# Hybrid decoder layers on one Trainium2 core: window attention moved beside the up projections, latent attention beside retention's projections, output weights prepared before retention's products

## The chip, the cores and the metric

The kernel runs on one core of one Trainium2 chip. The metric is the device time of one execution in microseconds (us). The kernel is a single launch; all weights come from device memory (HBM) during the execution.

## The reference, cut to what matters

Two decoder layers on 256 tokens of width 1024, all in float32. One input projection feeds three mixers; their outputs, concatenated, go through one output projection, a residual and a layer norm; then a router picks 2 of 16 experts for each token.

```python
(r_q, r_k, r_v, r_g, s_q, s_k, s_v, c_q, c_kv, k_rope) = jnp.split(x @ w_in[l], splits, axis=-1)
rq, rk = rope(r_q, pos), rope(r_k, pos)                      # 4 heads of 64
ret_o = retention(rq, rk, r_v, r_g, ret_gn_w[l])             # scores*decay, group norm, * silu(g)
swa_o = sliding_window_sink_attention(s_q, s_k, s_v, sinks)  # 6 query heads, 2 kv heads, band of 128
mla_o = latent_attention(c_q, c_kv, k_rope, ...)             # q = rms(c_q) @ w_uq; k,v = rms(c_kv) @ w_ukv
mix = jnp.concatenate([ret_o, swa_o, mla_o], -1) @ w_out[l]
x = layer_norm(ALPHA * x + mix, ...)
x = layer_norm(ALPHA * x + grouped_moe(x, ...), ...)         # 16 experts, 1024 -> 2x256 -> 1024, top 2
```

## The kernel before, in words

Tokens are two blocks of 128 (`t` = 0, 1). Every float32 product of the projections is done as three products of a shorter format: a weight chunk of 1024 columns is split into a high part (a rounding copy on ACT, L485) and a low part (a subtraction on DVE, L486), and `mm3` issues high·high (L497), low·high (L498) and high·low (L499). Buffers for the high parts are few, so a split waits until PE has finished with an earlier chunk. A block of input columns (`B4`, `B3`, `B2`, `B0`, `B1`) is one `project` of four chunks, 48 products of 512 columns where it is 512 wide.

The order in which the source writes the mixers of a layer is: `B4` (latent keys and values, window values), `B3` (latent queries), `B2` (window queries and keys; `ev2` copies them into `sqT` and the padded key tile `zpad`), the up projections from `w_uq` and `w_ukv` (36 products of 288 columns, then 18 of 256 and 12 of 384), q's transposes, three latent attentions, `B0` (retention's q and k with rotary positions, tile `rqk`), three window attentions, the load of the decay factors (`dec`, on ACT's DMA queue, L821), `B1` (retention's v and gate), retention itself, then the output projection, the routing and the experts.

One attention of two heads (`attend`) is a chain over three engines: PE scores into PSUM; DVE row maxima (L723); ACT exponentials (L729) and, for windows, the sink's (L734); DVE sums and reciprocal (L735, L736); DVE scaling of `p` (L739); PE transposes of `p` (L355); copies to `pt` on DVE and ACT (L213); PE products with the values (L745, L748); the copy into `mixT` in two parts (ACT L750, DVE L751).

Retention's chain is: rotary of `rqk` (DVE L508, L510, and an add on POOL, L511), eight transposes, copies to `rkT` and `zpad`, scores (L846, L847), DVE product with `dec` into `AT` (L849), inner products (L858), group norm (DVE L865, POOL's power L394, POOL's product of gate and scale L871, DVE L872), transposes of `ro`, `mixT`.

A scheduler decides the order of the instructions on each engine from the source and its own costs; each engine then runs its list strictly in the order shown in the next sections' listings. On PE this holds except in a guarded part (output projection, routing, experts), where the written order is kept. The output projection (`outp`, 96 products for both token blocks and both halves `j` of the columns) takes the eight blocks of `mixT` in the order of `order`, its weights' chunks in `OUT_ORDER`; retention's result is blocks 0 and 1, the windows' 2 to 4, latent's 5 to 7. Weights are requested from SP in one stream, with a limit (`pump(LIM[3])`) on how far.

Of the kernel before, what the change touches and what calls it, by code (L numbers as in the profile page):

```python
# [188 lines left out]
def hybrid_decoder_kernel(ctx: ExitStack, tc: tile.TileContext, x, w_in, ret_gn_w, swa_sinks,  # L189
# [86 lines left out]
    OUT_ORDER = (3, 2, 1, 0)  # L276
# [224 lines left out]
    def rope(o, i, cos, sin, nh, d):  # L501
# [9 lines left out]
        gp.tensor_tensor(o, o, tv, op=OP.add)  # L511
# [3 lines left out]
    def mixers(l):  # L515
# [149 lines left out]
        uqs = [split_w(wu, 576 * i, 576) for i in range(3)]  # L665
        for t in range(2):
            for hf in range(2):
                b = mis()
                for i in range(3):
                    mm3(P[:, b, :288], cqH[:, i, 128 * t:128 * t + 128], cqL[:, i, 128 * t:128 * t + 128],  # L670
                        uqs[i][0][:, 288 * hf:288 * hf + 288], uqs[i][1][:, 288 * hf:288 * hf + 288], i == 0, i == 2)
                qh = q[:, t, 3 * hf:3 * hf + 3]
                act.activation(qh, P[:, b, :288].rearrange("p (h d) -> p h d", d=96), AF.Copy, scale=rsq[:, t:t + 1])
                rope(qh[:, :, 64:96], qh[:, :, 64:96], kc(K_COSM + 32 * t, 32), kc(K_SINM + 32 * t, 32), 3, 32)

        uks = []
        for i, (o, ol) in enumerate(((1728, 3264), (2496, 1728))):
            h, lo = hchunk(768), wu.part(ol, ol + 768, F32R)
            w = wu.part(o, o + 768, F32).rearrange("p (h a d) -> p a h d", a=2, d=64)
            hv, lv = (y.rearrange("p (a h d) -> p a h d", a=2, d=64) for y in (h, lo))  # L680
            act.activation(hv, w, AF.Copy)
            dve.tensor_sub(lv, w, f_(hv))
            uks.append((h, lo))
        for pr in range(3):
            b = mis()
            for i in range(2):
                mm3(P[:, b, 0:256], uks[i][0][:, 128 * pr:128 * pr + 128], uks[i][1][:, 128 * pr:128 * pr + 128],
                    ckH[:, i], ckL[:, i], i == 0, i == 1)
            for u in range(2):
                copy(act if u else dve, kT[0:64, 2 * pr + u], P[64 * u:64 * u + 64, b, 0:256])  # L690
# [109 lines left out]

        for pr in range(3):
            window(pr)
        SV.free()
        SQT.free()


# [544 lines left out]
```

## Time and profile before

| | us |
|---|---|
| median of three runs | 526.99 (522.13 to 528.87) |
| the profiled execution | 521.82 |
| its span, first to last instruction | 519.9 |
| from the up projections to the routing, layer 0 / layer 1 | about 45 to 150 / 297 to 402 |
| experts, layer 0 / layer 1 | about 150 to 262 / 402 to 503 |

Times in the trace are counted from the start of the span. A line such as L355 is the line of the kernel that issued the instruction. `DVE` is VectorE, `ACT` ScalarE, `POOL` GpSimd, `SP` SyncE, `PE` TensorE.

### The profile page before, as it was taken

To read this page: it belongs to the slowest core of one execution; us is meant where nothing else is said; L and a number is where in the kernel's file an instruction comes from. 1 tells how busy PE (TensorE), PEld (TensorE's weight loads), DVE (VectorE), ACT (ScalarE), POOL (GpSimd) and SP (SyncE) were. 2 spreads that over 40 slices of the span, in tenths; PEclk is the share of its full clock that TensorE was granted. 3 is DMA by queue.
4 is the path that set the end of the run, shared out by engine and by line. 5 is a ranking of instruction groups with operands and counts; after the bars stand their busy time and mean duration, and the time that the engine had idled before them with its cause. 6 is when DMAs were issued, how large, how long until landed. Compare 5 with 4: busy or idle time off the path is not lost. (4 is left out here: it accounts for less than half of the span.)

```text
span 519.9 us, 8750 instructions
## 1 busy us (share of the span) xinstructions
PE 480.9 (92%) x3328; PEld 301.2 (58%) x3328; DVE 262.8 (51%) x713; ACT 199.4 (38%) x443; POOL 72.9 (14%) x74
## 2 busy tenths in 40 slices
PE   4999999788999999999989999977999999999984
PEld 3999877456855334243379987754677533523331
DVE  4565966855463132322487588576627501422136
ACT  4475754622343132221257485454124511421120
POOL 0022001002220019000003110100121100730000
PEclk9999999979999999999999999997999999999999
DMA  8999629540594999999989942547019779999982
GB/s 267 302 388 383 240 81 301 167 141 0 169 369 146 391 387 387 387 385 386 366 301 388 379 168 81 180 155 249 25 52 337 259 277 385 387 386 385 387 306 81
DMA packets 74164, 140.47 MB, mean 270 GB/s; under 512 B 4571, under 2 KB 11269, under 8 KB 74117
## 3 DMA queue, kind: packets, MB, share of 16 engines
q1 hardware_dynamic: 71264, 136.28, 73.3%
q10 hardware_dynamic: 2852, 3.58, 2.1%
q8 instruction: 28, 0.46, 0.4%
q14 instruction: 20, 0.16, 0.1%
HBM read 138.79 MB, written 1.05 MB: 269 GB/s over the span
## 5 line engine op out<-in xcount | busy, mean ns | idle before, releaser
L1111 PE MATMUL psum<-w_float,xg_float 128*32 128x512 f32 x1024 | 115.0, 594 | 2.1 <-DVE th L1119 2.1
L1111 PEld LDWEIGHTS psum<-w_float,xg_float 128*32 128x32 f32 x1024 | 31.6, 110 | 73.8 <-issue 67.6
L486 DVE TENSOR_TENSOR w_float32r<-w_float,h_r 128x1024 fp32r<-128x1024 f32 (+3 forms) x54 | 58.7, 1104 | 18.5 <-ACT h_r L485 18.4
L1130 PE MATMUL psum<-w_float,aT 128*32 128x512 f32 x512 | 58.4, 594 | 3.5 <-DMA w_float<-in_exp_w_down_dram 2.7
L485 ACT ACTIVATE h_r<-w_float 128x1024 fp32r<-128x1024 f32 (+3 forms) x54 | 51.0, 958 | 26.9 <-PE psum L499 12.4
L1140 DVE TENSOR_TENSOR ye_float32r<-psum,ye_float32r 128x512 fp32r<-128x512 f32 x28 | 19.2, 691 | 60.8 <-ACT ye_float32r L1139 60.8
L394 POOL TENSOR_TENSOR stats<-stats,small 128x1 f32<-128x1 f32 (+2 forms) x18 | 12.8, 710 | 222.8 <-DVE stats L393 222.7
L497 PE MATMUL psum<-h_r,xT_r 128*128 128x512 f32 (+1 forms) x96 | 38.3, 401 | 2.4 <-ACT h_r L485 1.5
L1130 PEld LDWEIGHTS psum<-w_float,aT 128*32 128x32 f32 x512 | 15.8, 110 | 42.1 <-issue 33.7
L499 PE MATMUL psum<-h_r,xT_r 128*128 128x512 f32 (+1 forms) x96 | 38.9, 407 | 0.8 <-DVE stats L393 0.8
L498 PE MATMUL psum<-w_float32r,xT_r 128*128 128x512 f32 (+1 forms) x96 | 38.7, 405 | 0.0
L1139 ACT ACTIVATE ye_float32r<-psum 128x512 fp32r<-128x512 f32 x28 | 16.5, 595 | 56.0 <-PE psum L1130 56.0
L1118 DVE SCALAR_TENSOR_TENSOR th<-th,psum 128x256 f32<-128x256 f32 x16 | 6.7, 421 | 58.1 <-ACT th L1117 58.1
L497 PE MATMUL psum<-xT_r,h_r 128*128 128x256 f32 x112 | 32.1, 288 | 0.0
L499 PE MATMUL psum<-xT_r,w_float32r 128*128 128x256 f32 x112 | 31.6, 284 | 0.0
L498 PE MATMUL psum<-xT_r,h_r 128*128 128x256 f32 x112 | 31.6, 283 | 0.0
L1117 ACT ACTIVATE th<-psum 128x256 f32<-128x256 f32 x16 | 6.1, 383 | 57.4 <-PE psum L1111 56.4
L498 PE MATMUL psum<-w_float32r,mixT_r 128*128 128x512 f32 x64 | 25.2, 394 | 0.0
L355 PE MATMUL psum<-ident_r,p 128*128 128x128 f32 x72 | 13.9, 305 | 10.7 <-DVE p L739 7.8
L729 ACT ACTIVATE p<-p,stats 128x128 f32<-128x128 f32 (+1 forms) x48 | 21.2, 445 | 4.9 <-DVE stats L726 4.9
L1084 ACT ACTIVATE xg_float<-psum,par 128x256 f32<-128x256 f32 x40 | 20.3, 564 | 5.6 <-PE psum L1080 4.9
L497 PEld LDWEIGHTS psum<-h_r,xT_r 128*128 128x128 f32 x96 | 18.7, 196 | 6.3 <-ACT h_r L485 1.9
(227 smaller groups left out, 907.6 us busy)
## 6 DMA issues: line engine op xcount, KB each, us to landing
w_float<-in_exp_w_gate_up_dram SPq DMA_DIRECT2D x64, 1024.0 KB
w_float<-in_exp_w_down_dram SPq DMA_DIRECT2D x32, 1024.0 KB
w_float<-in_w_in_dram SPq DMA_DIRECT2D x24, 512.0 KB
w_float<-in_w_out_dram SPq DMA_DIRECT2D x16, 512.0 KB
w_float<-in_w_in_dram SPq DMA_DIRECT2D x8, 384.0 KB
w_float<-in_w_in_dram SPq DMA_DIRECT2D x8, 288.0 KB
w_float<-in_mla_w_uq_dram SPq DMA_DIRECT2D x6, 288.0 KB
w_float<-in_mla_w_ukv_dram SPq DMA_DIRECT2D x4, 384.0 KB
```

The costliest lines, as they stand in the source:

```text
L355: pe.transpose(o, i, ident[:n, :n] if n != 128 else ident)
L485: first[0] = act.activation(h, w, AF.Copy)
L486: i = (e or dve).tensor_tensor(wl, w, f_(h), op=OP.subtract)
L497: pe.matmul(o, xh, wh, start=first, stop=False)
L498: pe.matmul(o, xh, wl, start=False, stop=False)
L499: pe.matmul(o, xl, wh, start=False, stop=last)
L729: act.activation(sb[u].v(a, z), sb[u].v(a, z), AF.Exp, bias=nb[:, c:c + 1], scale=scale, accum_out=sm[:, c:c + 1])
L1084: act.activation(xg[:, k], P[:, b, 0:256], AF.Identity, scale=g, bias=c)
L1111: pe.matmul(P[32 * e:32 * e + 32, 4 + t, :], xg[t][:, k, 4 * (g % 2) + e], w[:, 512 * e:512 * e + 512], start=k == 0, stop=k == 7, skip_gr ...
L1130: pe.matmul(P[32 * e:32 * e + 32, b, :], R.ATS[t].v(128 * f + 32 * e, 128 * f + 32 * e + 32), w[:, 512 * e:512 * e + 512], start=f == 0, s ...
L1139: act.activation(ys[0], P[:, b, :], AF.Copy)
L1140: last_ye[0] = dve.tensor_sub(ys[1], P[:, b, :], f_(ys[0]))
```

## The change

The windows come straight after `B2`, and the up projections after them in the source, using other PSUM banks (`acc()` in place of `mis()`), so that the scheduler may interleave both. The load of `dec` follows the windows. The latents now stand next to `B0`. Retention's transposes, scores and decay products come before `B1` in the source; the splits of all eight output-weight chunks (both halves) come after `B1` and before retention's inner products, and the output projection of token block 0 for `mixT`'s blocks 2 to 7 is taken out of the guarded part. The rotary add runs on DVE for the wide tiles; group norm's scale is multiplied into `ro` on DVE in place of into the gate on POOL. The transposed normed rows `x1T` get two buffers, and both of block 0's transposes (`turn`) stand together. No product is added or removed.

```diff
--- before.py
+++ after.py
@@ -273,7 +273,7 @@
     def width(blk):
         return sum(n for _, n in blk)
 
-    OUT_ORDER = (3, 2, 1, 0)
+    OUT_ORDER = (1, 2, 3, 0)
     stream = []
     for l in range(DEPTH):
         stream += [("in", l, B4), ("in", l, B3), ("u", l, 0), ("in", l, B2), ("in", l, B0), ("in", l, B1),
@@ -508,7 +508,7 @@
             dve.tensor_mul(tv[:, :, s * h:s * h + h], i[:, :, h - s * h:d - s * h],
                            sin[:, None, s * h:s * h + h].to_broadcast([128, nh, h]))
         dve.tensor_mul(o, i, cb)
-        gp.tensor_tensor(o, o, tv, op=OP.add)
+        (dve if nh * d >= 256 else gp).tensor_tensor(o, o, tv, op=OP.add)
         t2.free()
 
 
@@ -658,54 +658,6 @@
 
         project_T(B2, ev2)
 
-
-        wu = W[("u", l, 0)]
-        V = alloc(768, "mv", within=LAT)
-        v = V.ap.rearrange("p (t h d) -> p t h d", t=2, h=6)
...
-        wfree(("u", l, 0))
-
-
...
         MIX = alloc(4096, "mixT")
         mH, mL = MIX.v(0, 2048, 8, 256, r=True), MIX.v(2048, 4096, 8, 256, r=True)
 
@@ -752,15 +704,6 @@
             for x_ in sb + pts:
                 x_.free()
 
-        def latent(pr):
-            banks = [mis(), mis()]
...
         def window(pr):
             banks = [mis(), mis()]
             kvs = [(2 * pr + u) // 3 for u in range(2)]
@@ -772,6 +715,71 @@
                    [P[:, banks[1], 256 * u:256 * u + 256] for u in range(2)], banks, kc(K_WIN, 256), SWA_SCALE,
                    lambda u, t: sv[:, t, 64 * kvs[u]:64 * kvs[u] + 64], 2 * pr)
 
+
+        for pr in range(3):
+            window(pr)
+        SV.free()
+        SQT.free()
+        DEC = alloc(1024, "dec")
+        nc.scalar.dma_start(DEC.ap, const[:, K_DEC:K_DEC + 1024])
+
+
+        wu = W[("u", l, 0)]
+        V = alloc(768, "mv", within=LAT)
+        v = V.ap.rearrange("p (t h d) -> p t h d", t=2, h=6)
+        uqs = [split_w(wu, 576 * i, 576) for i in range(3)]
+        for t in range(2):
+            for hf in range(2):
+                b = acc()
...
+        for pr in range(3):
+            b = acc()
...
+        for t in range(2):
+            b = acc()
...
+        wfree(("u", l, 0))
+
+
+        QT = alloc(1536, "qT", within=LAT)
+        qT = QT.v(0, None, 6, 256)
+        for h0 in range(0, 6, 2):
+            b = mis()
...
+            copy(dve if h0 == 2 else act, qT[:96, h0:h0 + 2], P[:96, b].rearrange("p (a b) -> p a b", b=256))
+        FRONT.free()
+        def latent(pr):
+            banks = [mis(), mis()]
...
         for pr in range(3):
             latent(pr)
         LAT.free()
@@ -795,33 +803,9 @@
             rope(rqk[:, t].rearrange("p (h d) -> p h d", d=64), p.rearrange("p (h d) -> p h d", d=64),
                  kc(K_COSR + 64 * t, 64), kc(K_SINR + 64 * t, 64), 8, 64)
 
+
+        acc_i[0] = 0
         project(B0, ev0)
-
-
-        for pr in range(3):
-            window(pr)
-        SV.free()
-        SQT.free()
-
-
-        RV = alloc(512, "rv")
-        rv = RV.v(0, None, 2, 256)
-        RG = alloc(512, "rg")
-        rg = RG.v(0, None, 2, 256)
-
...
-        DEC = alloc(1024, "dec")
-        nc.scalar.dma_start(DEC.ap, const[:, K_DEC:K_DEC + 1024])
-        project(B1, ev1)
-        XHL.free()
-        pump(LIM[3])
 
 
         RKT = alloc(512, "rkT")
@@ -836,8 +820,6 @@
             for u in range(2):
                 copy(dve if u else act, qvv[64 * u:64 * u + 64, pr, 256 * u:256 * u + 256], P[64 * u:64 * u + 64, b, 0:256])
         RQK.free()
-        RO = alloc(512, "ro")
-        ro = RO.v(0, None, 2, 256)
         ATs = []
         for pr in range(2):
             AT = alloc(768, "AT")
@@ -849,6 +831,44 @@
             dve.tensor_mul(AT.v(0, 512), P[:, b0, :], DEC.v(512 * pr, 512 * pr + 512))
             dve.tensor_mul(AT.v(512, 768, 2, 128), P[:, b1, 0:256].rearrange("p (u i) -> p u i", u=2),
                            DEC.v(512 * pr, 512 * pr + 512).rearrange("p (u i) -> p u i", u=2)[:, :, 0:128])
+
+        RV = alloc(512, "rv")
+        rv = RV.v(0, None, 2, 256)
+        RG = alloc(512, "rg")
+        rg = RG.v(0, None, 2, 256)
+
+        def ev1(t, p):
...
+        project(B1, ev1)
+        XHL.free()
+
+
+        hb2 = alloc(4096, "h2")
+        order = (2, 3, 4, 5, 6, 7, 0, 1)
+        hs = {}
+
+        def split_out(j, n):
+            c = OUT_ORDER[n]
+            h, lo = split_w(W[("out", l, j)], 1024 * c, 1024,
+                            hb2.part(3072 - 1024 * n, 4096 - 1024 * n, F32R) if j else hb[0].v(1024 * n, 1024 * n + 1024, r=True))
+            for i in range(2):
+                hs[j, 2 * c + i] = h[:, 512 * i:512 * i + 512], lo[:, 512 * i:512 * i + 512]
+
+        for j in range(2):
+            for n in range(4):
+                split_out(j, n)
+        pump(LIM[3])
+
+
+        RO = alloc(512, "ro")
+        ro = RO.v(0, None, 2, 256)
+
         for t in range(2):
             b = mis()
             for h in range(4):
@@ -865,11 +885,11 @@
                 dve.bn_stats(bs, P[:, b, 64 * h:64 * h + 64])
                 dve.bn_aggr(mv[:, h], bs)
             rs = rstd(mv[:, :, 1], LN_EPS, 4)
-            o3, g3 = (y.rearrange("p (h d) -> p h d", d=64) for y in (ro[:, t], rg[:, t]))
+            o3 = ro[:, t].rearrange("p (h d) -> p h d", d=64)
             dve.tensor_tensor(o3, P[:, b, 0:256].rearrange("p (h d) -> p h d", d=64),
                               mv[:, :, 0:1].to_broadcast([128, 4, 64]), op=OP.subtract)
-            gp.tensor_tensor(g3, g3, rs[:, :, None].to_broadcast([128, 4, 64]), op=OP.mult)
             dve.tensor_mul(ro[:, t], ro[:, t], rg[:, t])
+            dve.tensor_tensor(o3, o3, rs[:, :, None].to_broadcast([128, 4, 64]), op=OP.mult)
             b = mis()
             for pr in range(2):
                 transpose(P[:, b, 128 * pr:128 * pr + 128], ro[:, t, 128 * pr:128 * pr + 128])
@@ -881,25 +901,9 @@
 
 
 
-        guard = tc.manual_schedule(engines={mybir.EngineType.PE})
-        guard.__enter__()
-        hb2 = alloc(4096, "h2")
-        R = Routing(l)
-        R.guard = guard
-        order = (6, 7, 5, 4, 2, 3, 0, 1)
-        hs = {}
-
-        def split_out(j, n):
...
-        def outp(t, j, part):
-            bk = 2 * t + j
-            for k in order[4 * part:4 * part + 4]:
-                mm3(P[:, bk, :], mH[:, k, 128 * t:128 * t + 128], mL[:, k, 128 * t:128 * t + 128],
+        def outp(t, j, a, z):
+            for k in order[a:z]:
+                mm3(P[:, 2 * t + j, :], mH[:, k, 128 * t:128 * t + 128], mL[:, k, 128 * t:128 * t + 128],
                     hs[j, k][0], hs[j, k][1], k == order[0], k == order[-1])
 
         def residue(t, j):
@@ -907,21 +911,22 @@
             dve.scalar_tensor_tensor(z, z, ALPHA, P[:, 2 * t + j, :], op0=OP.mult, op1=OP.add)
             ln_stats(t, j, z)
 
-        for n in range(4):
-            split_out(0, n)
-        outp(0, 0, 0)
-        outp(0, 0, 1)
-        residue(0, 0)
-        for n in range(4):
-            split_out(1, n)
-        outp(0, 1, 0)
+        for j in range(2):
+            outp(0, j, 0, 6)
+
+        guard = tc.manual_schedule(engines={mybir.EngineType.PE})
+        guard.__enter__()
+        R = Routing(l)
+        R.guard = guard
+        for j in range(2):
+            outp(0, j, 6, 8)
+            residue(0, j)
+        outp(1, 0, 0, 4)
         R.turn(0, 0)
-        outp(0, 1, 1)
-        residue(0, 1)
+        R.turn(0, 1)
+        outp(1, 0, 4, 6)
         R.products(0, 0)
-        outp(1, 0, 0)
-        R.turn(0, 1)
-        outp(1, 0, 1)
+        outp(1, 0, 6, 8)
         residue(1, 0)
         R.products(0, 1)
         hb[0].free()
@@ -929,9 +934,9 @@
         R.xg = alloc(4096, "xg")
         wfree(("out", l, 0))
         R.choose(0)
-        outp(1, 1, 0)
+        outp(1, 1, 0, 4)
         R.turn(1, 0)
-        outp(1, 1, 1)
+        outp(1, 1, 4, 8)
         residue(1, 1)
         R.products(1, 0)
         R.rank(0)
@@ -962,6 +967,7 @@
             self.ATS = [alloc(256, "aT", within=self.unit) for t in range(2)]
             self.XT = alloc(512, "x1T")
             self.x1 = [[self.XH[t].whole(F32R), Xb.part(1024 * t, 1024 * t + 1024, F32R)] for t in range(2)]
+            self.x1T = [y.part(0, 512, F32).rearrange("p (a b) -> p a b", b=128) for y in (self.XT, self.unit)]
             self.SM = [SMB.v(128 * t, 128 * t + 128) for t in range(2)]
             self.MK = [y.whole(BF) for y in MKB]
             self.bk = []
@@ -979,16 +985,16 @@
 
         def turn(self, t, j):
 
-            self.x1T = self.XT.v(0, None, 4, 128)
+            x1T = self.x1T[j]
             b = 2 + j if t else 4 + j
             for a in range(4):
                 transpose(P[:, b, 128 * a:128 * a + 128], X[t][:, 512 * j + 128 * a:512 * j + 128 * a + 128])
-            copy(act if HC[t][j] == "a" else dve, self.x1T, P[:, b].rearrange("p (a b) -> p a b", b=128))
+            copy(act if HC[t][j] == "a" else dve, x1T, P[:, b].rearrange("p (a b) -> p a b", b=128))
 
         def products(self, t, j):
 
             for k in range(4 * j, 4 * j + 4):
-                pe.matmul(P[:, 0 if t else 6, 0:16], self.x1T[:, k - 4 * j], rwg[:, k, 0:16], start=k == 0, stop=k == 7)
+                pe.matmul(P[:, 0 if t else 6, 0:16], self.x1T[j][:, k - 4 * j], rwg[:, k, 0:16], start=k == 0, stop=k == 7)
 
         def choose(self, t):
 
```

What the scheduler makes of it is seen in each engine's list. In these rows L713 stands for the windows' scores (L770 before), L697 and L700 for their products with the values (L745, L748 before), L828 and L829 for retention's scores (L846, L847 before), L702 and L703 for the copies into `mixT`, L843 and L844 for the gate's.

PE in the up projections, where before only products with `cT_r` stood in a row until the uk ones; now (the changed kernel, `p_47` and `p_48` are the first window's two heads):

```order
L713 MATMUL psum<-zpad_395,sqT_399 128x256
L713 MATMUL psum<-zpad_395,sqT_399 128x512
L713 MATMUL psum<-zpad_395,sqT_399 128x256
L713 MATMUL psum<-zpad_395,sqT_399 128x512
L499 MATMUL psum<-h_r,cT_r 128x288
...
L499 MATMUL psum<-h_r,cT_r 128x288
L355 MATMUL psum<-ident_r,p_47_526 128x128
L497 MATMUL psum<-h_r,cT_r 128x288
L355 MATMUL psum<-ident_r,p_47_526 128x128 x2
L355 MATMUL psum<-ident_r,p_48_532 128x128
```

Between the scores of two windows and the first window's transposes there are 19 products of 288 columns (left out but for the first and last); eight of the 36 stand ahead of the scores.

PE at retention, before. `p_78` to `p_83` belong to the second and third window, `xT_r` products are `B1`'s, `mixT_r` products the output projection's:

```order
L499 MATMUL psum<-h_r,xT_r 128x512
L770 MATMUL psum<-zpad_395,sqT_399 128x256
L355 MATMUL psum<-ident_r,p_78_901 128x128 x3
L355 MATMUL psum<-ident_r,p_79_907 128x128 x3
...
L355 MATMUL psum<-ident_r,rqk_786 128x128 x8
L355 MATMUL psum<-ident_r,p_82_939 128x128 x3
L355 MATMUL psum<-ident_r,p_83_945 128x128 x3
...
L847 MATMUL psum<-zpad_395,rkT_1057 128x256
L846 MATMUL psum<-zpad_395,rkT_1057 128x512 x2
```

and in the changed kernel:

```order
L355 MATMUL psum<-ident_r,rqk_902 128x128 x2
L498 MATMUL psum<-w_3072_4096_float32r,xT_r 128x512
...
L497 MATMUL psum<-h_r,mixT_r 128x512
L355 MATMUL psum<-ident_r,rqk_902 128x128 x6
L497 MATMUL psum<-h_96_3072_4096_float32r,mixT_r 128x512
L498 MATMUL psum<-w_1024_2048_float32r,mixT_r 128x512
...
L498 MATMUL psum<-w_2048_3072_float32r,mixT_r 128x512
L828 MATMUL psum<-zpad_395,rkT_977 128x512
L829 MATMUL psum<-zpad_395,rkT_977 128x256
```

After the last product of `B1` no window is left; six transposes of `rqk` follow one product of the output projection, and nine of its products stand between them and retention's scores.

DVE at the same place in the changed kernel (`w_..._362` and `w_..._356` are chunks of the output weights' first half, 0 and 1):

```order
L703 TENSOR_TENSOR mixT_r<-psum,mixT_r 128x256
L508 TENSOR_TENSOR rope_963<-psum,const_87 128x8x32 x2
L510 TENSOR_TENSOR rqk_902<-psum,const_87 128x512
L511 TENSOR_TENSOR rqk_902<-rqk_902,rope_963 128x512
L486 TENSOR_TENSOR w_0_1024_float32r<-w_0_1024_float_362,h_r 128x1024
L508 TENSOR_TENSOR rope_968<-psum,const_87 128x8x32 x2
L510 TENSOR_TENSOR rqk_902<-psum,const_87 128x512
L844 SCALAR_TENSOR_TENSOR tanh_1065<-tanh_1065,psum 128x256
L511 TENSOR_TENSOR rqk_902<-rqk_902,rope_968 128x512
L845 SCALAR_TENSOR_TENSOR rg_1003<-tanh_1065,gn_389 128x256
L486 TENSOR_TENSOR w_1024_2048_float32r<-w_1024_2048_float_356,h_r 128x1024
```

The add L511 is new on this list, and a split and the gate's L844 stand between the steps of the second rotary.

## Rows read from the trace of the kernel before

**Rows 1.** The page: its span, and the granted TensorE clock in 40 equal slices of the span (9 is 90% of full speed or more).

```profile
span 519.9 us, 8750 instructions
...
PEclk9999999979999999999999999997999999999999
```

**Rows 2.** Busy time of each engine in stretches of the span: start and end, length, then for each engine busy us and instructions, the granted clock, the share of the DMA engines' time and GB/s. Four stretches for the mixers of each layer and one for layer 0's experts.

```profile
45.20:91.10 45.90, 45.74 (x257) 36.84 (x255) 35.45 (x102) 28.17 (x66) 4.93 (x6) 1.00 0.67 234
91.10:105.90 14.80, 9.12 (x50) 5.49 (x49) 11.65 (x46) 9.22 (x33) 0.00 (x0) 0.96 0.57 193
105.90:111.60 5.70, 5.60 (x18) 3.59 (x19) 2.92 (x8) 1.26 (x3) 0.00 (x0) 0.50 0.38 116
111.60:150.10 38.50, 35.85 (x195) 28.68 (x193) 21.03 (x73) 10.75 (x20) 7.77 (x10) 1.00 0.39 133
...
342.60:357.90 15.30, 9.35 (x50) 5.50 (x50) 11.88 (x46) 9.39 (x33) 0.00 (x0) 0.98 0.56 197
357.90:364.10 6.20, 6.16 (x18) 3.86 (x19) 3.01 (x9) 1.64 (x4) 0.00 (x0) 0.50 0.40 115
364.10:402.00 37.90, 35.32 (x194) 28.59 (x192) 20.91 (x73) 10.36 (x19) 7.77 (x10) 1.00 0.39 130
150.10:262.00 111.90, 108.52 (x907) 42.29 (x906) 36.22 (x82) 31.23 (x68) 17.39 (x9) 1.00 0.98 357
```

**Rows 3.** PE's waits in layer 0's mixers (45.2 to 150.1 us): waiting line, the line waited for, total us, times, longest.

```profile
PE psum L355 <- DVE p L739: 3.9, 2, 2.5
PE psum L355 <- DVE ro L872: 1.5, 2, 1.0
PE psum L355 <- ACT h_r L485: 1.3, 1, 1.3
```

**Rows 4.** PE in order of time, layer 0, from the last product of `B1` on: start, us, line, operation; idle time before it and its releaser in brackets.

```profile
97.03 0.39 PE L499 MATMUL psum<-h_r,xT_r 128*128 128x512 f32 x1
97.26 0.59 PE L770 MATMUL psum<-zpad,sqT 128*128 128x256 f32 x2
99.22 1.13 PE L355 MATMUL psum<-ident_r,p 128*128 128x128 f32 x6 [1.37 <-DVE p L739]
...
102.79 0.66 PE L355 MATMUL psum<-ident_r,rqk 128*128 128x128 f32 x4 [0.35 <-DVE mixT_r L751]
105.99 1.56 PE L355 MATMUL psum<-ident_r,p 128*128 128x128 f32 x6 [2.54 <-DVE p L739]
```

**Rows 5.** The second window's chain on DVE and then on ACT, in order of time.

```profile
94.52 0.34 DVE L723 CUSTOM_DVE_ANT_0 p<-psum,const,par 128x128 f32<-128x128 f32 x1
...
98.38 0.17 DVE L735 TENSOR_TENSOR stats<-stats 128x4 f32<-128x4 f32 x1 [1.15 <-ACT stats L734]
...
98.79 1.01 DVE L739 TENSOR_SCALAR p<-p,stats 128x128 f32<-128x128 f32 x4
```

```profile
96.39 0.39 ACT L729 ACTIVATE p<-p,stats 128x128 f32<-128x128 f32 x1
...
98.15 0.19 ACT L734 ACTIVATE stats<-stats 128x4 f32<-128x4 f32 x1
```

**Rows 6.** The end of `B2` and the start of the up projections, in order of time: PE, DVE, ACT; and the two stretches of the up projections in the form of Rows 2.

```profile
45.22 0.30 PE L497 MATMUL psum<-h_r,cT_r 128*128 128x288 f32 x1
45.35 0.29 PE L498 MATMUL psum<-w_float32r,cT_r 128*128 128x288 f32 x1
```

```profile
45.81 0.94 DVE L682 TENSOR_TENSOR w_float32r<-w_float,h_r 128x768 fp32r<-128x768 f32 x1
46.79 0.43 DVE L213 COPY zpad<-psum 64x256 f32<-64x256 f32 x1
```

```profile
47.25 0.38 ACT L213 ACTIVATE zpad<-psum 64x256 f32<-64x256 f32 x1
```

```profile
45.20:50.00 4.80, 4.80 (x39) 4.80 (x38) 3.45 (x13) 3.27 (x8) 0.78 (x2) 1.00 1.05 387
50.00:54.95 4.95, 4.95 (x34) 4.44 (x33) 4.80 (x11) 3.96 (x8) 1.57 (x2) 1.00 0.95 349
```

**Rows 7.** Groups of instructions by line and shape, 40 to 150 us: count, busy us and mean ns, and idle time before them with releasers. DVE, then ACT, then POOL.

```profile
L486 DVE TENSOR_TENSOR w_float32r<-w_float,h_r 128x1024 fp32r<-128x1024 f32 x12 | 14.8, 1231 | 2.3 <-ACT h_r L485 2.3
...
L508 DVE TENSOR_TENSOR rope<-psum,const 128x256 f32<-128x256 f32 x4 | 1.6, 420 | 1.8 <-POOL rqk L511 1.5 <-PE psum L748 0.3
...
L849 DVE TENSOR_TENSOR AT<-psum,dec 128x512 f32<-128x512 f32 x2 | 1.4, 686 | 1.0 <-PE psum L847 1.0
L510 DVE TENSOR_TENSOR rqk<-psum,const 128x512 f32<-128x512 f32 x2 | 1.4, 681 | 0.0
L508 DVE TENSOR_TENSOR rope<-mq,const 128x48 f32<-128x48 f32 x8 | 1.3, 203 | 1.2 <-ACT mq L673 0.6 <-POOL mq L511 0.6
```

```profile
L485 ACT ACTIVATE h_r<-w_float 128x1024 fp32r<-128x1024 f32 x12 | 12.6, 1054 | 5.4 <-PE psum L499 5.1 <-ACT p L729 0.2
```

```profile
L511 POOL TENSOR_TENSOR rqk<-rqk,rope 128x512 f32<-128x512 f32 x2 | 2.6, 1291 | 30.6 <-DVE rqk L510 30.6
L511 POOL TENSOR_TENSOR mq<-mq,rope 128x96 f32<-128x96 f32 x4 | 2.3, 587 | 7.4 <-DVE mq L510 6.6 <-ACT h_r L681 0.8
```

**Rows 8.** Transfers: a stretch at the start of layer 0's experts, in the form of Rows 2; and SP's requests for the output weights in layer 0, in order of time.

```profile
160.00:166.00 6.00, 5.89 (x49) 3.31 (x53) 2.35 (x7) 2.70 (x8) 0.00 (x0) 1.00 0.01 3
```

```profile
40.06 7.26 SPq L308 DMA_DIRECT2D w_float<-in_w_out_dram  x8
```

More of the change, by code (lines that the diff above doesn't have):

```diff
@@ L676, in mixers @@
[L676 to L683, printed above, removed]
-        for pr in range(3):
[L685 to L690, printed above, removed]
@@ L708, in mixers @@
-        FRONT.free()
         MIX = alloc(4096, "mixT")
@@ new lines, in mixers @@
+        uks = []
+        for i, (o, ol) in enumerate(((1728, 3264), (2496, 1728))):
+            h, lo = hchunk(768), wu.part(ol, ol + 768, F32R)
+            w = wu.part(o, o + 768, F32).rearrange("p (h a d) -> p a h d", a=2, d=64)
+            hv, lv = (y.rearrange("p (a h d) -> p a h d", a=2, d=64) for y in (h, lo))
+            act.activation(hv, w, AF.Copy)
+            dve.tensor_sub(lv, w, f_(hv))
+            uks.append((h, lo))
+        for pr in range(3):
+            b = acc()
+            for i in range(2):
+                mm3(P[:, b, 0:256], uks[i][0][:, 128 * pr:128 * pr + 128], uks[i][1][:, 128 * pr:128 * pr + 128],
+                    ckH[:, i], ckL[:, i], i == 0, i == 1)
+            for u in range(2):
+                copy(act if u else dve, kT[0:64, 2 * pr + u], P[64 * u:64 * u + 64, b, 0:256])
@@ new lines, in mixers @@
+        FRONT.free()
+        def latent(pr):
+            banks = [mis(), mis()]
+            for u in range(2):
+                h, b = 2 * pr + u, banks[u]
+                pe.matmul(P[:, b, 0:128], qT[:96, h, 0:128], kT[:96, h, 0:128], start=True, stop=True)
+                pe.matmul(P[:, b, 128:384], qT[:96, h, 128:256], kT[:96, h, :], start=True, stop=True)
+            attend(5 + pr, [P[:, b, 0:128] for b in banks], [P[:, b, 128:384] for b in banks], banks, kc(K_CM, 256), MLA_SCALE,
+                   lambda u, t: v[:, t, 2 * pr + u, :])
@@ L851, in mixers @@
                            DEC.v(512 * pr, 512 * pr + 512).rearrange("p (u i) -> p u i", u=2)[:, :, 0:128])
+        RV = alloc(512, "rv")
[3 more added lines that the diff above has]
+        def ev1(t, p):
+            copy(act, rv[:, t], p[:, 0:256])
+            th = alloc(256, "tanh")
+            act.activation(th.ap, p[:, 256:512], AF.Tanh, scale=0.5)
+            dve.scalar_tensor_tensor(th.ap, th.ap, 1.0, p[:, 256:512], op0=OP.add, op1=OP.mult)
+            dve.scalar_tensor_tensor(rg[:, t], th.ap, 0.5, gnb.ap, op0=OP.mult, op1=OP.mult)
+            th.free()
+        project(B1, ev1)
[7 more added lines that the diff above has]
+                            hb2.part(3072 - 1024 * n, 4096 - 1024 * n, F32R) if j else hb[0].v(1024 * n, 1024 * n + 1024, r=True))
+            for i in range(2):
+                hs[j, 2 * c + i] = h[:, 512 * i:512 * i + 512], lo[:, 512 * i:512 * i + 512]
[5 more added lines that the diff above has]
+        ro = RO.v(0, None, 2, 256)
         for t in range(2):
```

56 lines of the change are left out of this document (13 added, 43 removed).

## The prediction, made before the changed kernel ran

> **What bounds the kernel now.** I read the page first: the TensorE clock is below full speed in only a few of the 40 slices [rows 1]. The table of stretches then shows where PE lost time. From 45 to 91 us it is busy without a gap, while the transfers and the other engines are not at their limits. From 91 to 150 us it is not [rows 2]. The list of waits names the causes: 3.9 us for scaled rows `p` of the windows, 1.5 us for `ro`, 1.3 us for a split's high part [rows 3]. PE's own sequence shows why: once `B1`'s last product is out at 97.26, two windows and retention follow one another with nothing between, so 1.37 and 2.54 us pass with PE waiting [rows 4]. In the stretch after that the granted clock is 0.50, so that all 5.6 us of work in it take twice as long [rows 2]. So the change is aimed at a stretch in which a DVE/ACT chain ends last, not PE.
>
> **What can be given back.** Layer 0: 14.80 − 9.12 = 5.68 us idle, then 5.70 − 5.60 = 0.10, half of 5.60 = 2.80 for the clock, and 38.50 − 35.85 = 2.65 around retention and the output projection, in all 11.2 us. Layer 1 by the same sum: 5.95 + 0.04 + 3.08 + 2.58 = 11.7 [rows 2]. Together 22.9 us, and no more, since the change removes no product. The new order must be worth 22.9 us less the waits that it makes itself. I walked the lists of the changed kernel by hand with durations of these rows. Per layer:
>
> (a) *Windows 0 and 1 inside the up projections.* Their cover is the up projections' 9.7 us of products [rows 6]. The first wait is certain in kind: window scores need `zpad`, whose last copy starts on ACT at 47.25 us and ends at 47.63, since it follows a DVE copy at 46.79 that stands behind a 0.94 us split [rows 6]. PE is there at 46.98: eight products of 0.13 us after 45.22 end at 46.3, and the first window's scores take 0.6. That is 0.7 us. Next, from DVE's first maximum to PE's first transpose a window took 99.22 − 94.52 = 4.7 us [rows 4, 5], from 47.2 here, so 51.9; PE has 0.6 us of scores and 19 × 0.13 = 2.5 us, ending at 50.8: 1.1 us. The second window's chain starts behind the first's copies and a 0.95 us split, and I find 0.6 us there. Sum 2.4, bounds 0.6 (the scheduler's gaps fill) to 4.0 (no product of the second window's cover in time).
>
> (b) *`B0`'s start.* Its first low half stands on DVE behind the third window's maxima and three copies, and takes 1.23 us [rows 7]; PE has two products (0.46 us) ahead. 1.0, bounds 0.5 to 2.5, the latter two splits' time.
>
> (c) *The third window's transposes* behind two such splits on DVE, with 11 products × 0.23 = 2.5 us of cover (0.23 from 97.03 to 97.26 [rows 4]). 0.6, bounds 0 to 1.5.
>
> (d) *q's rotary and transposes.* Four pieces, each two products and a sum on DVE and a POOL add of 0.59 us [rows 7], are now late, behind a split of `B1`. DVE waited for this POOL add before already. 1.2, bounds 0.5 to 2.5.
>
> (e) *The second `rqk`.* On DVE between the last latent's `mixT` and PE's six transposes stand a rotary (2 × 0.42 + 0.68 + 0.68 = 2.2 us), a split (1.23), a second rotary's first three steps (1.5), the gate's L844 that waits for `B1`'s end (0.4) and the add (0.68): 6.0 us, and 0.8 for `mixT`'s own copies. The add is at 0.68 since DVE's 128x512 product costs that; POOL took 1.29 [rows 7]. PE has some 21 products, 4.8 us. 2.0, bounds 1.0 to 3.5.
>
> (f) *Retention's scores.* Three splits of output weights stand on ACT (3 × 1.05 us) ahead of the copies to `rkT` and `zpad`, and two on DVE [rows 7]; nine products of 0.23, 2.1 us, cover part. 0.9, bounds 0 to 2.0.
>
> (g) *The rest*: latents, `ro`, routing. `ro` alone cost 1.5 us [rows 3]; now twenty products of the output projection stand before its first transposes. 0.7, bounds 0.3 to 1.5.
>
> Sum 8.8 us a layer (2.9 to 17.5). Gain 11.4 − 8.8 = 2.6 a layer, 5.3 in all.
>
> **Edits at nothing.** `dec` loaded earlier: before, the decay product waited 1.0 us for PE's scores, not for the transfer [rows 7], so 0; it is one instruction on ACT's list at a place where ACT waits for PE. Output weights arrive long before: all are requested from 40 to 47 us [rows 8], and `B1` alone ends at 97 [rows 4]. Group norm's scale on DVE: a product of 0.42 for a POOL one, hidden under the output projection [rows 7]; if that cover is gone, 0.4 for each token block. The second buffer of `x1T` and `turn` together: PE has products before and after, 0 (0 to 0.4).
>
> **Expert stage.** The experts run with transfers at 0.98 share [rows 2], so an earlier start of PE helps only if the transfers start earlier too. They do: for 6 us at the start of the experts nothing is moved [rows 8], since the buffers are all full and free up as the first expert's products are done. If mixers end 2.6 us earlier, so does that, and the stage moves as a whole.
>
> [...]
> [...]
>
> **Forecast.** The sum is made against the profiled execution, 521.8 us; the median of the three runs is 527.0, 1.0% above. 521.8 − 5.3 = 516.5, times 1.01 is **521.6 us**. Its own range, with (a) and (e) off by 1.5 us a layer each: 515 to 528. A change within 2% (10.5 us) is about what a measurement of this kernel can't tell from none. Chance 0.44.
>
> **Rivals.**
> 1. *The waits nearly vanish*, at their lower bounds: 2.9 a layer, gain 8.5, 17.1 in all: 504.7, on the median's scale **509.7**. For it: DVE is busy 35 of 46 us and ACT 28 in 45 to 91, so an added window of about 5 us on each would fit [rows 2], and chains start earlier than I walk if the splits do. Against: (a)'s first wait and (e) stand in the lists themselves. Chance 0.23.
> 2. *The clock falls again* after (e): the 2.80 and 3.08 us are lost as before. 516.5 + 5.9 = 522.4, **527.6**. For it: 0.50 in both layers after such a gap. Against: after the change products surround each gap. Chance 0.14.
> 3. *Slower: DVE's list holds the chains up.* Ten splits of 1.23 us stand between steps of the window, rotary and retention chains on DVE, and each would delay PE by its length: 12.3, with (a)'s 2.4 and (g)'s 0.7 and the clock's 2.9, 18.3 us a layer against 11.4. It loses 6.9 a layer: 521.8 + 13.8 = 535.6, **540.9**. It is slower from the point at which waits and clock pass 11.4 us a layer. For it: the split ahead of `zpad` [rows 6]. Against: most splits have 2.5 us of `B0`'s or `B1`'s products each, twice their length. Chance 0.11.
> 4. *The gain does not come through*, because the expert stage is timed by transfers that start no earlier: **527**. Against it, the 6 us without transfers. Chance 0.08.
>
> **How the numbers follow.** The likeliest case gives 521.6. Range 509 to 531: it leaves out most of rival 3 and the fast half of rival 1, near 0.2. Faster by over 2% (below 516.4): rival 1 and the lower end of the forecast's range, 0.32. Slower (over 537.5): rival 3 in most of its width, 0.09. Within: 0.59.
>
> **What would show it.** PE's waits from the up projections to the experts should sum to about 9 us a layer, with entries for `zpad` copies and `p` in the first 10 us, for `rqk` near 2 us, and for low halves (L486) near 1; no wait for `dec`. The granted clock should be 1.00 in all stretches of the mixers. The experts' stretch of layer 0 should keep its 112 us [rows 2]. Wrong would be: a clock of 0.50 after the latents (rival 2), DVE without idle time while PE waits for several of its lines (rival 3), or waits below 4 us a layer (rival 1).

## The result, and the profile after

The changed kernel takes 506.4 us (506.36 to 507.61, four runs) against 526.9 us: a ratio of 0.963, 95% interval 0.956 to 0.970. The profiled execution is 506.46 us. A few executions that ran slow as a whole are left out of every ratio: one of dec_only below (560.0 us at a mean granted clock of 0.843), three of clock_fill and one of the kernel before. The forecast had the sign right and the size wrong: 521.6 us was forecast, its range ended at 509. The page of after, span and granted clock [rows 1]:

```profile
span 504.7 us, 8736 instructions
...
PEclk9999999999999999999999999999999999999998
```

The span is 15.2 us shorter. Where, is read from PE's first gathering product behind the routing, which ends the mixers of a layer. Before, in layers 0 and 1, then after:

```profile
147.17 0.35 PE L1080 MATMUL psum<-oh_r,x1H_r 128*128 128x256 f32 x1 [0.95 <-DVE route L1045]
...
399.09 0.36 PE L1080 MATMUL psum<-oh_r,x1H_r 128*128 128x256 f32 x1 [0.94 <-DVE route L1045]
```

```profile
139.93 0.38 PE L1086 MATMUL psum<-oh_r,x1H_r 128*128 128x256 f32 x1 [0.85 <-DVE oh_r L1042]
...
383.75 0.39 PE L1086 MATMUL psum<-oh_r,x1H_r 128*128 128x256 f32 x1 [0.85 <-DVE oh_r L1042]
```

Layer 0 gives 7.2 us, layer 1 another 8.1, and from there to the end both kernels need the same (120.8 and 120.9 us). The up projections of layer 1 start 149.6 and 149.9 us behind the routing of layer 0 (before, then after):

```profile
296.73 0.30 PE L497 MATMUL psum<-h_r,cT_r 128*128 128x288 f32 x1
```

```profile
289.78 0.30 PE L497 MATMUL psum<-h_r,cT_r 128*128 128x288 f32 x1
```

So everything is won in the mixers, and the expert stages move as a whole. PE's stretch of layer 0 from the up projections to the experts, and its waits in it [rows 2, 3]:

```profile
45.20:143.10 97.90, 93.40 (x521) 73.46 (x523) 72.61 (x232) 49.30 (x122) 8.96 (x12) 1.00 0.56 197
```

```profile
PE psum L497 <- ACT h_r L485: 1.4, 1, 1.4
PE psum L355 <- POOL mq L511: 1.0, 1, 1.0
PE psum L497 <- ACT mv L213: 0.9, 1, 0.9
PE psum L1086 <- DVE oh_r L1042: 0.9, 1, 0.9
PE psum L498 <- DVE w_float32r L486: 0.2, 1, 0.2
```

4.5 us idle at the full clock, where before it was 8.6 us idle and 2.8 us lost to the clock. PE at the first two windows' scores, at the first one's transposes and at three of those waits, in order of time; then DVE's second rotary add, and the split's high part on ACT that PE waited for:

```profile
46.37 2.88 PE L713 MATMUL psum<-zpad,sqT 128*128 128x256 f32 x8
48.69 0.69 PE L499 MATMUL psum<-h_r,cT_r 128*128 128x288 f32 x1
...
51.48 0.29 PE L499 MATMUL psum<-h_r,cT_r 128*128 128x288 f32 x1
51.82 0.30 PE L355 MATMUL psum<-ident_r,p 128*128 128x128 f32 x1
...
64.07 0.50 PE L497 MATMUL psum<-h_r,xT_r 128*128 128x512 f32 x1 [0.89 <-ACT mv L213]
...
74.75 0.32 PE L355 MATMUL psum<-ident_r,mq 128*96 128x128 f32 x1 [0.96 <-POOL mq L511]
...
105.20 0.50 PE L497 MATMUL psum<-h_r,mixT_r 128*128 128x512 f32 x1 [1.42 <-ACT h_r L485]
105.54 0.82 PE L355 MATMUL psum<-ident_r,rqk 128*128 128x128 f32 x6
```

```profile
104.67 0.68 DVE L511 TENSOR_TENSOR rqk<-rqk,rope 128x512 f32<-128x512 f32 x1
```

```profile
104.10 1.05 ACT L485 ACTIVATE h_r<-w_float 128x1024 fp32r<-128x1024 f32 x1
```

### The profile page after: what moved, and what is told of

Same layout as the page of the kernel before. It is cut to its first block, busy times and chain, and to the rows that moved or that the text cites. A ratio compares the mean times of both kernels' runs of the same rounds, so it can differ in the third digit from the quotient of the medians.

```text
span 504.7 us, 8736 instructions
## 1 busy us (share of the span) xinstructions
PE 474.5 (94%) x3328; PEld 298.3 (59%) x3328; DVE 265.3 (53%) x721; ACT 198.7 (39%) x443; POOL 65.4 (13%) x66
## 3 DMA queue, kind: packets, MB, share of 16 engines
HBM read 138.79 MB, written 1.05 MB: 277 GB/s over the span
## 5 line engine op out<-in xcount | busy, mean ns | idle before, releaser
L486 DVE TENSOR_TENSOR w_float32r<-w_float,h_r 128x1024 fp32r<-128x1024 f32 (+3 forms) x54 | 58.4, 1098 | 17.7 <-ACT h_r L485 17.6
L498 PEld LDWEIGHTS psum<-xT_r,h_r 128*128 128x128 f32 x112 | 21.5, 192 | 0.0
```

Source lines behind the costliest of these rows:

```text
L486: i = (e or dve).tensor_tensor(wl, w, f_(h), op=OP.subtract)
L498: pe.matmul(o, xh, wl, start=False, stop=False)
```

## The experiments

All times are medians of timed executions; ratios are to the kernel before, run beside each on the same chip. "The changed kernel" is 506.4 us; no variant ran beside it. The fastest execution of the kernel before lies between 521.5 and 522.1 us in all five sets, so a difference of 2 us to the changed kernel can be read, one below 1 us cannot. Line numbers differ a little from kernel to kernel; the operation and the tiles name the instruction. The diffs are cut to the lines that matter.

**Is it the windows?** Two kernels: only the windows moved, and everything but the windows moved.

```diff
 # win_only: the kernel before
+        for pr in range(3): window(pr)      # behind project_T(B2, ev2); up projections on acc()
...
-        for pr in range(3): window(pr)      # behind project(B0, ev0)
```

> The kernel before with one edit: the three windows stand behind B2, beside the up projections (which take the other PSUM banks); retention, the splits of the output weights and everything later stay as they were. Theory A (moving the windows and latents to where products stand beside them is the gain; the rest is trimming): the two p waits and the low clock go, about 4 us of waits and 2.8 to 3.1 us of clock a layer against 1 to 2 us of new waits, so 10 to 13 us less than before, within 3 us of the changed kernel's 506.4. Theory B (without early output weights and early retention scores the waits only move behind B1 and the clock falls again): 516 or more.

520.7 us, ratio 0.989 (0.983 to 0.995). Theory B's range, and its signs: in layer 0 PE waits for POOL's rotary adds of `rqk`, and the clock falls in the stretch behind them (second fence: 106 to 112 us):

```profile
PE psum L355 <- POOL rqk L511: 4.8, 2, 3.0
```

```profile
106.00:112.00 6.00, 3.78 (x12) 3.30 (x13) 3.60 (x7) 2.49 (x8) 2.17 (x1) 0.59 1.05 396
```

Retention's rotary chain took the place of the windows' chains as the next thing with no products beside it.

```diff
 # win_back: the changed kernel
-        for pr in range(3): window(pr)      # behind project_T(B2, ev2)
...
         project(B0, ev0)
+        for pr in range(3): window(pr)
```

> The changed kernel with the windows put back behind B0, everything else as changed: the output weights are split early, so that the last windows can be mixed with products of the output projection. Theory A: the windows' chains are again late; most of the gain is lost, 515 or more. Theory C (what mattered is that products of the output projection are ready to fill PE beside the last chains, wherever the windows stand): at most 3 us of the gain is lost, 506 to 510, and the granted clock stays at 1.00 in the mixers.

504.4 us (503.4 to 505.9), ratio 0.959 (0.953 to 0.965): no gain is lost, and the median is 2 us under the changed kernel's. That is what theory C expects, not A. The windows are as late as before, and PE still has work beside them; its waits in layer 0 name no window but for 0.2 us:

```profile
PE psum L497 <- ACT h_r L485: 0.9, 1, 0.9
PE psum L1087 <- DVE oh_r L1043: 0.9, 1, 0.9
PE psum L498 <- DVE w_float32r L486: 0.5, 1, 0.5
PE psum L497 <- ACT mixT_r L898: 0.5, 1, 0.5
PE psum L697 <- DVE pt L213: 0.2, 1, 0.2
```

Between the second window's transposes and the third's stand twelve products of the output projection (the `mixT_r` rows; the first and the last of them are shown, between the two windows' transposes):

```profile
96.92 0.38 PE L355 MATMUL psum<-ident_r,p 128*128 128x128 f32 x2
98.23 0.50 PE L497 MATMUL psum<-h_r,mixT_r 128*128 128x512 f32 x1 [0.93 <-ACT h_r L485]
...
103.92 0.39 PE L499 MATMUL psum<-h_float32r,mixT_r 128*128 128x512 f32 x1
104.50 0.30 PE L355 MATMUL psum<-ident_r,p 128*128 128x128 f32 x1 [0.20 <-ACT h_float32r L485]
```

So here the DVE and ACT chains of a window cost PE next to nothing beside products of the output projection; they do not need the up projections for it.

**Is it the output weights?**

```diff
 # late_split: the changed kernel
-        for j in range(2):
-            for n in range(4): split_out(j, n)      # behind project(B1, ev1)
...
-        for j in range(2): outp(0, j, 0, 6)         # outside the guard
...
+        for n in range(4): split_out(0, n)          # in the guard, as before
+        outp(0, 0, 0, 8); residue(0, 0)
+        for n in range(4): split_out(1, n)
+        outp(0, 1, 0, 8); residue(0, 1)
```

> The changed kernel with the output weights' splits and the first token block's output projection written as before, inside the guarded part behind retention. Theory A: 506 to 509, since retention's chain is short. Theory C: retention's transposes and scores lose their cover, 2 to 4 us a layer come back, 511 or more.

512.9 us, ratio 0.978 (0.971 to 0.984): 6.5 us come back. Of them 2.9 are named: retention's `ro` ends last again (0.7 in layer 0, 2.2 in layer 1), with layer 1's mean clock at 0.98. But the edit hardly changed what it was meant to change: the scheduler still puts the first output products ahead of retention's scores, the first of them at 105.42 us (105.20 in the changed kernel). So the run does not say what these products are worth there.

```profile
PE psum L355 <- DVE ro L889: 2.9, 2, 2.2
```

```profile
105.42 0.50 PE L497 MATMUL psum<-h_r,mixT_r 128*128 128x512 f32 x1 [1.42 <-ACT h_r L485]
```

```diff
 # out_only: win_back, and also
-        (dve if nh * d >= 256 else gp).tensor_tensor(o, o, tv, op=OP.add)
+        gp.tensor_tensor(o, o, tv, op=OP.add)
...
-        nc.scalar.dma_start(DEC.ap, ...)            # behind the windows
+        nc.scalar.dma_start(DEC.ap, ...)            # ahead of RKT
```

> The changed kernel with the windows put back behind B0, all rotary adds on POOL and the decay factors requested late: what is left of the change are the early splits of the output weights, the early first token block of the output projection, retention's scores written ahead of B1, the latents beside B0 and the small edits behind retention. Theory C (products of the output projection ready beside the last chains are the gain): 506 to 512, with the clock at 1.00 except behind a wait for the decay load. Theory A: 518 or more.

508.2 us (508.2 to 508.4), ratio 0.971 (0.965 to 0.977), clock 0.996. So what is left here holds most of the gain by itself, 14 us against the 522.3 us of the kernel before beside it. That is a bundle: the early splits, the early first block of the output projection and its new order of blocks, retention's scores written ahead of `B1`, and the small edits behind retention. No run takes it apart. In particular, every variant below 514 us has retention's scores written ahead of `B1` and none above has, so that edit is a rival to the output products that is not excluded.

**Decay factors and rotary adds**, undone one at a time:

```diff
 # late_dec: the changed kernel          # pool_add: the changed kernel
+  DEC load ahead of RKT                 +  gp.tensor_tensor(o, o, tv, op=OP.add)
```

> The changed kernel with the decay factors requested later, right ahead of retention's copies on ACT's list. In the run with filled gaps the decay product waited 4.1 us for this transfer and PE 3.8 us behind it. Theory D (the early load pays as soon as retention comes early): 3 to 5 us a layer come back, 512 to 516, with a wait of the decay product for the transfer. Theory E (my step: worth nothing): 506 to 507.

510.2 us (508.1 to 511.3), 3.7 more than the changed kernel. Theory D in kind; the size lies between the theories, since only layer 1 waits (DVE row). PE is busy for half of the next stretch, and then the granted clock is at 0.50 (354 to 357 and 357 to 364 us):

```profile
354.94 0.69 DVE L832 TENSOR_TENSOR AT<-psum,dec 128x512 f32<-128x512 f32 x1 [2.50 <-DMA dec<-in_const_dram]
```

```profile
354.00:357.00 3.00, 1.43 (x9) 1.18 (x9) 2.06 (x3) 0.00 (x0) 0.00 (x0) 1.00 0.02 7
357.00:364.00 7.00, 7.00 (x28) 6.33 (x27) 5.49 (x21) 0.00 (x0) 0.92 (x1) 0.50 0.30 85
```

> The changed kernel with all rotary adds on POOL as before. In the run with only the windows moved PE waited 4.8 us in layer 0 for two POOL adds of 2.1 us. If the add's move to DVE is a load-bearing part: 3 to 5 us a layer, 512 to 516, and a clock below full speed behind it. If PE's waiting for the first output split (1.4 us) hides it: 506 to 508.

508.3 us (507.6 to 508.7): 1.9 more, at the edge of the second expectation. PE waits 3.0 us for POOL's `rqk` adds over both layers, the granted clock is 0.70 from 105.9 to 111.6 us, and layer 0's wait for the first output split (1.4 us) is gone in exchange.

**Retention's chain with the windows away:**

```diff
 # win_rope: win_only, and also
+        (dve if nh * d >= 256 else gp).tensor_tensor(o, o, tv, op=OP.add)
```

> The kernel before with two edits: the windows beside the up projections and the wide rotary add on DVE. Theory F (windows leave a gap behind B1 in which retention's rotary chain, then the late decay load, end last; both must go): the two waits for POOL vanish, but the decay product waits for its load, 512 to 518. Theory A (windows and rotary are all there is): 505 to 509.

516.2 us, ratio 0.984 (0.978 to 0.991). The range of theory F, but not its cause: the scheduler has the decay load early here, and what ends last is `ro`, 5.2 us in both layers. Take the adds away, and the group norm is next.

**What is the clock worth?** Products that nothing reads, in the gaps:

```diff
 # clock_fill: the kernel before
         project(B1, ev1)
+        for i in range(18):
+            pe.matmul(P[:, 1, :], XH[:, 0, 0:128], XHL.v(0, 512, r=True), start=True, stop=True)
 # clock_fill2: the same with the DEC load ahead of the latents
```

> The kernel before with 18 products of 512 columns added to each layer that nothing reads (4.1 us of PE work a layer at the full clock), placed by the scheduler in the gaps behind B1: 7 ahead of the second window's transposes, 2 among them, 9 behind its products. If the lost clock was paid for as I reckoned (2.8 and 3.1 us), the stretch behind the gap runs at the full clock and the kernel is 4 to 6 us faster than before although it does more work; if the clock's loss only overlaps with waits, the same or up to 4 us slower.

531.5 us, ratio 1.011 (1.006 to 1.015). The gap is filled and the clock in it stays at 1.00 (91 to 108 us), yet the kernel is slower: the decay factors come late. Request on ACT's queue, then DVE:

```profile
107.64 0.33 ACTq L821 DMA_DIRECT2D dec<-in_const_dram  x1
```

```profile
114.34 0.69 DVE L851 TENSOR_TENSOR AT<-psum,dec 128x512 f32<-128x512 f32 x1 [4.09 <-DMA dec<-in_const_dram]
```

So the experiment didn't answer its question, and found the next one. With the load early:

> The filled kernel again (before, plus 18 products of 512 columns a layer that nothing reads), now with the decay factors loaded early, so that their transfer can't be the next thing late. If the clock's loss is paid as reckoned, the stretch behind the gap now runs at 1.00 and the kernel is 3 to 6 us faster than before in spite of 8 us more PE work. If filling only delays the chains: 526 or more.

514.6 us, ratio 0.982 (0.975 to 0.988). Its control is the early load alone:

```diff
 # dec_only: the kernel before           # rope_only: the kernel before
+  DEC load ahead of the latents         +  (dve if nh * d >= 256 else gp).tensor_tensor(...)
 # dec_rope: both
```

> The kernel before with one edit: the decay factors loaded ahead of the latents. With both edits (this and the wide rotary add on DVE) it gained 7 us or more, and with this edit and 18 idle products 8 or more. If the early load does it alone (it lets the scheduler put retention's copies and scores elsewhere, and keeps the transfer out of the gap): 513 to 517, and the idle products and the adds are worth nothing in the kernel before. If the low clock or the POOL adds were the payers: 521 to 527 as before.

> The kernel before with one edit: the wide rotary adds on DVE. PE's list stays as it was. If the adds pay by themselves: 515 to 518. If not, 521 to 528 and the two waits for p as before.

> The kernel before with two edits alone: the decay factors loaded ahead of the latents, the wide rotary adds on DVE. In the kernel before neither is waited for by PE, so both theories C and D give no gain on their own: 522 to 528, with the same two waits for p and the low clock. If they are worth something by themselves: 518 or less.

| | us | ratio (95%) |
|---|---|---|
| dec_only | 516.9 | 0.987 (0.982 to 0.992) |
| rope_only | 522.6 | 0.998 (0.994 to 1.002) |
| dec_rope | 515.5 | 0.986 (0.979 to 0.993) |
| dec_only with 18 idle products (clock_fill2) | 514.6 | 0.982 (0.975 to 0.988) |

The early load alone gives 5.7 us, the adds alone nothing. With the idle products it is 2 us less again, on another chip and with an overlapping interval: 8 us more work (18 products of 0.23 us in each layer) costs nothing. Part of it stands in time in which PE was idle (2.4 us in the first of these stretches), and the granted clock is higher in both; how much of the 8 us each pays is not separated. The stretches 98.0 to 105.9 and 105.9 to 111.6 us, of dec_only and then of clock_fill2:

```profile
98.00:105.90 7.90, 5.49 (x31) 3.18 (x30) 5.34 (x21) 3.68 (x13) 0.00 (x0) 0.89 1.02 358
105.90:111.60 5.70, 3.98 (x10) 2.06 (x8) 3.81 (x9) 2.20 (x7) 0.00 (x0) 0.55 0.16 58
```

```profile
98.00:105.90 7.90, 7.90 (x50) 6.10 (x49) 5.63 (x22) 4.12 (x13) 0.00 (x0) 1.00 0.56 174
105.90:111.60 5.70, 4.12 (x10) 2.05 (x9) 3.81 (x9) 2.11 (x7) 0.00 (x0) 0.71 0.85 314
```

How the early load pays in the kernel before is not settled: the decay product there didn't wait for the transfer [rows 7], and moving one request also made the scheduler put retention's copies and scores in another order.

**A faster kernel?** Edits against the largest waits that are left:

```diff
 # best: the changed kernel
-        (dve if nh * d >= 256 else gp).tensor_tensor(o, o, tv, op=OP.add)
+        dve.tensor_tensor(o, o, tv, op=OP.add)
...
         uqs = [split_w(wu, 576 * i, 576) for i in range(3)]
+        acc_i[0] = 3
...
-   hb[0].v(1024 * n, 1024 * n + 1024, r=True)
+   hb[0].v(1024 * ((n + 1) % 4), 1024 * ((n + 1) % 4) + 1024, r=True)
 # wb_best: win_back with the first and the third of these
```

> The changed kernel with three edits against its three largest waits: all rotary adds on DVE (1.0 us a layer for q's add on POOL), the up projections' PSUM banks shifted so that B0's first bank is free (0.9), and the first output chunk split into the buffer that is free first (1.4). If the waits are independent: 5 to 6 us less than the changed kernel, 500 to 502. If each only uncovers the chain behind it, as with the windows back: 504 to 506.

502.3 us (501.5 to 503.6), ratio 0.960 (0.953 to 0.966): about 4 us under the changed kernel, just above the first expectation, and the lowest time of all. The three waits are gone; smaller ones took their place. Layer 0:

```profile
PE psum L1087 <- DVE oh_r L1043: 0.9, 1, 0.9
PE psum L497 <- ACT kT L213: 0.5, 1, 0.5
PE psum L497 <- ACT mixT_r L898: 0.5, 1, 0.5
```

> The changed kernel with the windows put back behind B0 and two further edits: all rotary adds on DVE, and the first output chunk split into the buffer that comes free first (its high part stood behind the gate's copies, with PE waiting 1.4 us for it). Both waits should go, 2 to 4 us less than with the windows back alone (504.4): 500 to 502. If those waits only uncover the next ones: 504.

504.5 us, against 504.4 without the two edits: there they give nothing. A wait of 1.4 us for a split's low half (L486) stands in layer 0 in their place.

## Why the prediction was wrong

*What bounds the kernel, and the 22.9 us that can come back*: right in kind. 15.3 us came back in the profiled execution, all of it between `B2` and the experts.

*The sum of new waits* is the step that failed: 8.8 us a layer. By the profile PE is idle for 4.5 us in layer 0, and by the span the new order costs 11.2 − 7.2 = 4.0. That took the profiled execution 10 us below the forecast's 516.5; the factor to the median, below, makes the other 5. Term by term, in layer 0:
- (a) 2.4, measured about 1.7. From the start of the scores (46.37 us) to the first transposes (51.82) 5.45 us passed, where I had walked 46.3 to 51.9. So the first two waits were right together, 1.8 against 1.7, and only divided otherwise: PE was late from the scores on (its last product ahead of the transposes starts at 51.48, not 50.7) and had 0.2 us left to wait. Most of this waiting is inside the modelled durations of PE's rows and not in its idle time. The second window's 0.6 was not there.
- (b) 1.0, measured 0.9, but released by ACT's copy of `mv`, which frees `B0`'s PSUM bank, not by a split.
- (c) 0.6: none. The third window's transposes had their cover.
- (d) 1.2, measured 1.0, released by POOL's add as said. Its 0.59 us was a mean of unlike adds: the one that PE waited for took 1.28 us, the other three 0.39 (last section).
- (e) 2.0, measured 1.4 and 0.2, from another instruction: the first output split's high part, behind the gate's copies on ACT. That stop covered the wait for `rqk`, which I had named: its add started at 104.67 us and took 0.68, and PE's transposes began at 105.54, with no wait of their own.
- (f) 0.9: none. The first of the three splits on ACT that I had put behind the transposes ran during PE's stop (from 104.10 us).
- (g) 0.7, measured 0.9 for the routing's one-hot rows, as before.

These are 6.1 us against 8.8. In (c), (e) and (f) I took PE's earliest arrival, and added up. A PE that has waited once comes late to the next chain, whose engines have gone on meanwhile: the waits for a split and for `rqk` in (e) and for the copies in (f) were one wait, not two or three. This is read from the rows; no run tested it alone. The other 2 us, from 6.1 to 4.0, are mostly a matter of counting. At the full clock PE's busy time in these stretches is the same in both kernels (93.5 and 93.4 us), so about as much waiting hides in the modelled durations of the kernel before, and the 11.2 us left it out; where it stands there is not located.

*The edits at nothing*: wrong for the decay load. It is worth 3.7 us in the changed kernel. In the kernel before, moving it gave 5.7, by a way that stays open. I had looked only at who waited in the kernel before, where PE and the clock were later still. Group norm's scale and the second buffer of `x1T` were in no run by themselves. The rotary add was in (e), at 0.68 us for POOL's 1.29, so 1.2 over both layers; pool_add shows 1.9 in the changed kernel, and rope_only nothing in the kernel before.

*The factor to the median*: wrong. I multiplied by 1.01. The change removes most of what made the median longer than the profiled execution. Thirteen executions of the kernel before on one chip go by their mean granted clock: 521.9 to 523.3 us at 0.985 or 0.986, 525.3 at 0.983, 525.0 at 0.980, and 526.4 to 527.1 at 0.977 to 0.973. The changed kernel's four runs lie at 0.994 to 0.997 and within 1.3 us. So 15.2 us is the gain over the kernel before at its best, and 20 over its median.

*The expert stage* moved as a whole, as said: rival 4 is out. *Rival 2*, the clock: the mixers of the changed kernel run at 1.00, with no wait above 1.4 us in layer 0, but in win_only (0.59, after waits of up to 3.0 us) and late_dec (0.50, after 3.0 us in which PE was busy for 1.43) the low clock is back behind PE's waits. How long a wait it takes, no run shows. *Rival 3*, splits in the chains: they do stand there, but PE waited 1.6 us behind splits in layer 0, where their length was 12.3. *Rival 1*, 509.7 us, was nearest, and still 3 us too long, by the factor: its 504.7 us in the profiled execution's terms is 1.8 us under the 506.5 measured.

What I had not seen at all is which part pays. I read the change as windows finding cover in the up projections. win_back shows that they need not move, win_only that moving them alone gives 5 us, and out_only that the rest holds 14. In the lists this rest shows as products of the output projection beside the last chains. That it is these products that pay, and not retention's scores written ahead of `B1`, is argued from the lists and not shown.

## What to carry to other kernels

Ask which products can be made ready early enough to stand beside the last chains; here the windows' chains could stay where they were (win_back). When waits that follow one another on one engine are costed, carry PE's delay on from one to the next instead of summing each from its earliest arrival, and don't scale a gain by a median that the change itself moves. An edit that frees nothing in the kernel before (a load, an add) can be the next limit once the wait in front of it is gone, so try it in both kernels.

## What the runs showed of the hardware that I had not expected

POOL's rotary add of 128x512 took 1.29 us in the kernel before [rows 7], and 2.1 us in win_only, where a DVE split of 1.2 us was running as each began. POOL's rows, then DVE's:

```profile
102.45 2.08 POOL L511 TENSOR_TENSOR rqk<-rqk,rope 128x512 f32<-128x512 f32 x1 [25.67 <-DVE rqk L510]
106.00 2.17 POOL L511 TENSOR_TENSOR rqk<-rqk,rope 128x512 f32<-128x512 f32 x1 [1.47 <-DVE rqk L510]
```

```profile
102.20 1.22 DVE L486 TENSOR_TENSOR w_float32r<-w_float,h_float32r 128x1024 fp32r<-128x1024 f32 x1
...
105.83 1.22 DVE L486 TENSOR_TENSOR w_float32r<-w_float,h_r 128x1024 fp32r<-128x1024 f32 x1
```

The same is behind (d): in the changed kernel q's adds of 128x96 take 0.39 us, but the second, which begins during a split, takes 1.28, and PE waits for it. POOL, then DVE:

```profile
72.22 0.39 POOL L511 TENSOR_TENSOR mq<-mq,rope 128x96 f32<-128x96 f32 x1 [28.18 <-DVE mq L510]
73.41 1.28 POOL L511 TENSOR_TENSOR mq<-mq,rope 128x96 f32<-128x96 f32 x1 [0.80 <-DVE mq L510]
```

```profile
73.22 1.23 DVE L486 TENSOR_TENSOR w_float32r<-w_float,h_r 128x1024 fp32r<-128x1024 f32 x1
```

In each of the three the add took 0.8 to 0.9 us longer, and the split did not (1.22 to 1.23).

And a transfer of half a megabyte (`dec`, 128x1024 float32) took 6.7 us from request to use in clock_fill, 107.64 to 114.34 us, where weights stream (DMA share 1.05 from 108 to 110 us, first row). In the kernel before it was requested at 109.83, with the DMA engines idle (0.01, second row), and used at 113.45; DVE had waited for PE there, so the transfer took at most 3.6 us:

```profile
108.00:110.00 2.00, 2.00 (x7) 0.95 (x5) 1.44 (x4) 0.77 (x2) 0.00 (x0) 1.00 1.05 401
108.00:110.00 2.00, 2.00 (x9) 1.28 (x8) 0.00 (x0) 0.37 (x2) 0.00 (x0) 0.50 0.01 3
```

```profile
109.83 0.34 ACTq L821 DMA_DIRECT2D dec<-in_const_dram  x1
```

```profile
113.45 0.69 DVE L849 TENSOR_TENSOR AT<-psum,dec 128x512 f32<-128x512 f32 x1 [1.01 <-PE psum L847]
```
